# A depthwise convolution on TensorE: two output positions per product, and input copies made of one run per partition

## The chip, the cores and the metric

The kernel runs on one core of one Trainium2 chip. The metric is the device time of one execution in microseconds; before the change three runs gave a median of 1752.48 us (1751.03 to 1752.51). Of one further execution the hardware profiler kept a trace, from which every other time below is taken.

## The reference

One step of a diffusion backbone on 384 tokens (128 of context, 256 of latent) with 1024 channels, in four layers; every layer is a mixer and an MLP. The change touches only the mixer of the second layer, a conformer convolution module:

```python
def _conformer_conv(h, w_pw1, b_pw1, dw_w, dw_b, ln_g, ln_b, w_pw2, b_pw2):
    val, gate = jnp.split(h @ w_pw1 + b_pw1, 2, axis=-1)
    z = val * jax.nn.sigmoid(gate)
    z = _dwconv_centred(z, dw_w, dw_b)          # 31 taps along the tokens, per channel
    z = jax.nn.silu(_layernorm(z, ln_g, ln_b))
    return z @ w_pw2 + b_pw2
```

The two segments of tokens are convolved apart, each padded with zeros. All arithmetic is in float32.

## The kernel before

Channels lie on the 128 partitions in eight tiles (0 to 7), tokens along the free axis; between the two segments is a gap of zeros, so that a tile is 399 columns wide for the convolution. `conformer` goes through the tiles so:

- `pwin(m)` is the product pw1 of tile m, 48 matmuls of 128x128 by 384 columns (value and gate, each with split weights), and `glu(m)` after it: two activations on ScalarE (L834, L835) and a product on VectorE into the padded tile `zp` (L847). Products 0 and 1 come out of the normalisation's own stage, 2 to 7 follow; the text calls them pw2 to pw7.
- Tiles 0 and 1 are convolved on VectorE (`conv_dve`, one instruction of 399 columns per tap, L903), tile 1 in two pieces: 20 taps between pw6 and pw7, the rest after pw7.
- Tiles 2 to 7 are convolved on TensorE (`conv_mm`). A matmul contracts over 128 rows that are 4 shifts of 32 channels; its weights are 32 columns of diagonals from `diag`. Eight steps of four taps, for four groups of 32 channels, make 32 matmuls of 399 columns for a tile. The shifted rows, `z4`, come through DRAM: `zp` is stored to `zd` (L854), and four copies (L857) each fill 32 partitions of `z4` with four runs of 1.7 KB per partition, shifted by one column each. `dg` (L861) brings the tile's 512 KB of diagonals. Stores and copies of tiles 2 to 5 are issued by GpSimd, those of tiles 6 and 7 by SP (`SYNCZ`), which also issues all weight loads, in the order of the program. `z4` has three buffers; `dg` shares three with the modulation weights `dmw`.
- A convolved tile goes from PSUM straight to `zc` with its bias: on ScalarE (L885) for the four tiles in `FIRST`, whose mean over channels `mu` (`shift`) is taken away afterwards, on VectorE (L887) for the others, which subtract `mu` at once. `moments` adds each tile to the running sums for the layer norm.
- Tile 7 is convolved inside `stats`, in 256 and 128 columns; each part is followed by the products `lnm` and `lnv` with ones, which end the sums over channels. Then `normed` normalises all tiles, and the projection pw2 of the module (`out_proj`, product `p`) begins.

An engine takes its instructions in the order of the program, and waits at each until its semaphores are there; that holds for the queues that issue transfers too. A transfer issued by SP or ScalarE signals its landing on one of eight counters (DMAHW0 to DMAHW7 in the orders below), one issued by GpSimd on one of eight others (DMASW0 to 7).

## Time and profile before

| | |
|---|---|
| median of three runs | 1752.48 us |
| the profiled execution | 1750.85 us, with a span of 1748.7 us from the first instruction to the last |
| mean granted clock of TensorE | 0.997 |
| busy, share of the span | TensorE 99%, VectorE 80%, ScalarE 54%, GpSimd 1% |
| moved | 316.69 MB read from HBM, 3.96 MB written, 183 GB/s over the span |
| the convolution on TensorE | group of 448 matmuls, 32.8 us |
| the conformer's stretch from pw2 to the projection | 473.7 to 568.8 us |

Busy time is the time in which an engine had an instruction under way. A row of a timeline gives start, duration, engine, line, operation and tiles (equal neighbours as one row with their count), and in brackets how long the engine was idle ahead of it and what ended that. A row on transfers gives the KB of each and the median time from its issue to its landing. In the windows' table each engine has its busy microseconds and, in brackets, its instructions; then come the clock granted to TensorE (1.00 is full), the busy share of the DMA engines, and what they moved.

### The profile page before, as it was taken

The page shows a single profiled execution, that of the slowest core. Times are in us where ns is not written, and L with a number is a line of the kernel's source. Part 1 is how long each engine was busy: PE and PEld are TensorE (multiplying, and loading weights), DVE is VectorE, ACT ScalarE, POOL GpSimd, SP SyncE. Part 2 cuts the span into 40 slices and gives each one's busy share as a digit, 9 for nine tenths or more (in the row PEclk, how much of TensorE's full clock was granted, in tenths as well). Part 3 has the DMA queues.
Part 4 walks back from the last instruction along what each step waited for, and adds up shares of the span by engine and source line. Part 5 has one row for each costly group of instructions (what it writes and reads, how often), then busy time and mean ns, then how long its engine had stood idle before and what let it go on. Part 6 is the DMA issues. An engine that isn't in the chain of part 4 may idle for free.

```text
span 1748.7 us, 27296 instructions
## 1 busy us (share of the span) xinstructions
PE 1723.2 (99%) x10442; PEld 1625.2 (93%) x10442; DVE 1404.8 (80%) x2791; ACT 945.0 (54%) x1697; POOL 16.1 (1%) x36
## 2 busy tenths in 40 slices
PE   8999999999999999999999999999999999999997
PEld 7779999999986999999987889999999789999997
DVE  5998999899897898889875668889999978843443
ACT  4876672454633774254465657524546976733531
POOL 0000000000020000000000000000000000000000
PEclk9999999999999999999999999999999999999999
DMA  9665367766486247767554433676774413533331
GB/s 389 236 219 177 128 225 254 239 246 236 159 237 180 97 139 259 240 219 241 195 182 140 133 99 130 205 240 235 242 241 162 155 49 121 174 128 121 124 135 43
DMA packets 67795, 322.42 MB, mean 184 GB/s; under 512 B 7952, under 2 KB 13456, under 8 KB 44496
## 3 DMA queue, kind: packets, MB, share of 16 engines
q1 hardware_dynamic: 66384, 316.30, 52.8%
q0 software_dynamic: 1280, 4.38, 1.0%
q8 instruction: 82, 1.34, 0.3%
q14 instruction: 49, 0.40, 0.1%
HBM read 316.69 MB, written 3.96 MB: 183 GB/s over the span
## 4 chain that ended last, share of the span: by engine, by line
PE 77%; DVE 15%; ACT 3%; issue 2%; DMA 2%; SPq 0%; DVEq 0%; ACTq 0%
PE f L131 29%; PE o L131 27%; PE pw L131 4%; PE lo L131 3%; DVE mjunk L331 3%; PE qk L131 3%; DVE wlo L219 2%; PE p L131 2%; PE wo L131 2%; PE cps L131 2%; PE v L131 2%; DVE xf L608 1%; DMA pmw<-wmod 1%; PE s L131 1%; PE po L131 1%
## 5 line engine op out<-in xcount | busy, mean ns | idle before, releaser
L218 ACT ACTIVATE whi<-raw 128x1024 fp32r<-128x1024 f32 x360 | 378.5, 1059 | 545.3 <-PE o L131 327.2
L219 DVE TENSOR_TENSOR wlo<-raw,whi 128x1024 fp32r<-128x1024 f32 x360 | 437.7, 1221 | 165.6 <-ACT whi L218 165.3
L331 DVE SCALAR_TENSOR_TENSOR mjunk<-dmw,condb 128x1024 bf16<-128x1024 f32 x308 | 375.3, 1219 | 1.5
L131 PE MATMUL o<-hl,whi 128*128 128x384 f32 x1024 | 343.0, 335 | 0.0
L131 PE MATMUL o<-hh,wlo 128*128 128x384 f32 x1024 | 343.0, 335 | 0.0
L131 PE MATMUL o<-hh,whi 128*128 128x384 f32 x1024 | 343.0, 335 | 0.0
L131 PEld LDWEIGHTS o<-hh,wlo 128*128 128x128 f32 x1024 | 192.2, 188 | 0.0
L131 PEld LDWEIGHTS o<-hh,whi 128*128 128x128 f32 x1024 | 192.2, 188 | 0.0
L131 PEld LDWEIGHTS o<-hl,whi 128*128 128x128 f32 x1024 | 192.2, 188 | 0.0
L501 DVE SCALAR_TENSOR_TENSOR x<-o,modv,x 128x128 f32<-128x128 f32 (+1 forms) x128 | 47.4, 412 | 69.0 <-PE o L131 69.0
L131 PE MATMUL g<-xf,graw 128*128 128x386 f32 x256 | 85.7, 490 | 1.7 <-DVE gl L666 1.7
L131 PEld LDWEIGHTS g<-xf,graw 128*128 128x128 f32 x256 | 47.9, 190 | 34.3 <-DVE gl L666 2.3
L785 DVE TENSOR_TENSOR hl<-s,hh 128x384 fp32r<-128x384 f32 x128 | 71.1, 555 | 6.6 <-ACT s L784 2.4
L783 ACT ACTIVATE hh<-r 128x384 fp32r<-128x384 f32 x128 | 67.1, 524 | 3.3
L784 ACT ACTIVATE s<-r 128x384 f32<-128x384 f32 x128 | 65.2, 509 | 0.0
L779 ACT ACTIVATE r<-f 128x384 f32<-128x384 f32 x112 | 53.0, 473 | 13.4 <-PE f L131 13.4
L131 PE MATMUL lo<-yh,wlo 128*128 128x384 f32 x128 | 43.5, 340 | 1.6 <-DVE wlo L219 1.6
L131 PE MATMUL lo<-yl,whi 128*128 128x384 f32 x128 | 43.0, 336 | 0.0
L131 PE MATMUL lo<-yh,whi 128*128 128x384 f32 x128 | 42.6, 336 | 0.0
L903 DVE SCALAR_TENSOR_TENSOR zt<-zp,vec,zt 128x399 f32<-128x399 f32 x58 | 36.7, 633 | 1.4
L131 PE MATMUL wo<-oT,whi 128*128 128x384 f32 x128 | 33.7, 343 | 0.0
L131 PE MATMUL cps<-z,dg 128*32 128x399 f32 (+2 forms) x448 | 32.8, 449 | 0.0
(1515 smaller groups left out, 4002.2 us busy)
## 6 DMA issues: line engine op xcount, KB each, us to landing
raw<-wst SPq DMA_DIRECT2D x180, 1024.0 KB, 5.0
dmw<-wmod SPq DMA_DIRECT2D x154, 512.0 KB, 4.1
pmw<-wmod SPq DMA_DIRECT2D x34, 512.0 KB, 6.8
graw<-wst SPq DMA_DIRECT2D x16, 512.0 KB, 4.8
bt<-rpbt SPq DMA_DIRECT2D x16, 384.0 KB, 3.5
z<-zd POOLq DMA_DIRECT2D x16, 213.5 KB, 6.7
dg<-diag SPq DMA_DIRECT2D x6, 512.0 KB, 4.1
pmwl<-wmod SPq DMA_DIRECT2D x4, 512.0 KB, 5.0
```

The costliest lines, as they stand in the source:

```text
L131: i = nc.tensor.matmul(*a, **kw)
L218: nc.scalar.activation(hi, raw[:, s], AF.Copy)
L219: nc.vector.tensor_tensor(lo, raw[:, s], hi.bitcast(F32), op=ALU.subtract)
L331: nc.vector.scalar_tensor_tensor(mjunk, w, 0.5, condb[:, s], op0=ALU.mult, op1=ALU.mult, accum_out=mod_tile(l)[:, c, m, s:s + 1]))
L501: nc.vector.scalar_tensor_tensor(x[m][:, xa:xb], ps[:, a:b], mv[:, g, m, s:s + 1], x[m][:, xa:xb], op0=ALU.mult, op1=ALU.add)
L608: nc.vector.scalar_tensor_tensor(xf, r[:, k:k + LG], lcw[:, j, t, k:k + 1], xf, op0=ALU.mult, op1=ALU.add)
L779: nc.scalar.activation(r, ps[:, :N], AF.Relu)
L783: nc.scalar.activation(hh, r, AF.Square)
L784: nc.scalar.activation(s, r, AF.Square)
L785: nc.vector.tensor_tensor(hl, s, hh.bitcast(F32), op=ALU.subtract)
L903: nc.vector.scalar_tensor_tensor(t, z[:, k:k + CG], dww[:, m, k:k + 1], t, op0=ALU.mult, op1=ALU.add)
```

## The change

Tile 0 stays on VectorE. Tile 1 moves to TensorE, and tiles 1 to 6 (`PAIR_CONV`) get a new form, `conv_pair`: a matmul contracts over 8 shifts of 16 channels, and its 32 output rows are those 16 channels at two neighbouring positions. It has 200 columns (one for each pair of positions), and four steps for eight groups of 16 channels make 32 matmuls for a tile. The weights come from a new input `pairw`. `glu` writes even and odd positions apart; the store to `zd` takes both halves. Channel c*8+g of a tile now sits in row c of group g, so that what a partition of `z4` needs, eight groups one behind the other, is one run of 6.9 KB in DRAM. Eight copies of 16 partitions, one for each shift, fill `z4`. Tile 7 (`LAST`) keeps the old matmuls, but its channels are dealt likewise, and its four copies are of 32 partitions with one run of 6.9 KB each. The rows of the weights, biases and gains that follow are put in the same order ahead of the launch.

The result of a pair product has two positions of a channel on two partitions. ScalarE copies it from PSUM to `co` (L917), four transfers issued by ScalarE (L920, 51 KB each) bring both positions onto one partition in `zq`, and `conv_in` moves it to `zc` (ScalarE for tiles 0 to 3, now in `FIRST`, VectorE for the others). The mean is taken ahead of the end of pw7, three pair products stand ahead of pw6, and three behind pw7. SP issues the copies of tile 5 too.

```diff
-CG = SEQ + 15 + LAT
-CSEG = ((0, 0, SEQ), (1, SEQ + 15, CG))
-CP = CG + CW
-PE_CONV = (2, 3, 4, 5, 6, 7)
+CGAP = 16
+CG = SEQ + CGAP + LAT
+CSEG = ((0, 0, SEQ), (1, SEQ + CGAP, CG))
+CP = CG + CW + 1
+PAIR_CONV = (1, 2, 3, 4, 5, 6)
+LAST = 7
 TAP = CW // 4 + 1
-SYNCZ = (6, 7)
-CONVCUT = 20
+SYNCZ = (5, 6, 7)
 ZW = CG + 4 * (TAP - 1)
+CU = CG // 2
+PV = CU + 15
+PZ = CU + 12
+ZB = 2 * (PV + 1) + 8
+ZT = 3 * CP + ZW
+PT = 7 * PV + PZ
...
-FIRST = (2, 3, 0, 4)
+FIRST = (0, 1, 2, 3)
...
                 for s, a, b in SEG:
-                    o = 15 + 15 * s
-                    i = nc.vector.scalar_tensor_tensor(z[:, a + o:b + o], th[:, a:b], 1.0, v[:, a:b],
-                                                       op0=ALU.add, op1=ALU.mult)
+                    o = 15 + CGAP * s
+                    dst, p, q = z[:, a + o:b + o], th[:, a:b], v[:, a:b]
+                    if m in PAIR_CONV:
+                        o = a // 2 + 8 * s
+                        dst = z[:, 7:7 + 2 * PV + 2].rearrange("p (f v) -> p f v", f=2)[:, :, o:o + (b - a) // 2]
+                        p, q = (t.rearrange("p (v f) -> p f v", f=2) for t in (p, q))
+                    i = nc.vector.scalar_tensor_tensor(dst, p, 1.0, q, op0=ALU.add, op1=ALU.mult)
                 glus.append(i.ins)
-                if m in PE_CONV:
-                    z4 = cp.tile([P, 4, ZW], F32, tag="z4", name=f"z4{l}{m}", bufs=3)
-                    zd = dp.tile([P, CP], F32, tag="zd", name=f"zd{l}{m}", bufs=3)
-                    dma = (nc.sync if m in SYNCZ else nc.gpsimd).dma_start
-                    dma(zd, z)
-                    zg = zd.rearrange("(g c) n -> c g n", g=4)
-                    for s in range(4):
-                        i = dma(z4[32 * s:32 * s + 32], zg[:, :, s:s + ZW])
+                dma = (nc.sync if m in SYNCZ else nc.gpsimd).dma_start
+                if m == LAST or m in PAIR_CONV:
+                    z4 = cp.tile([P, ZT], F32, tag="z4", name=f"z4{l}{m}", bufs=3)
+                    dg = wp.tile([P, D], F32, tag="dmw", name=f"dg{l}{m}", bufs=3)
+                    if m == LAST:
+                        zd = dp.tile([P, CP], F32, name=f"zd{l}{m}")
+                        dma(zd, z[:, :CP])
+                        zr = zd.rearrange("(c g) n -> c (g n)", g=4)
+                        for t in range(4):
+                            i = dma(z4[32 * t:32 * t + 32], zr[:, t:t + ZT])
+                        z4 = [z4[:, g * CP:g * CP + ZW] for g in range(4)]
+                        dg = dg.rearrange("p (t n) -> p t n", t=TAP)
+                        nc.sync.dma_start(dg, diag)
+                    else:
+                        zd = dp.tile([2, P, PV], F32, tag="zd", name=f"zd{l}{m}", bufs=3)
+                        dma(zd.rearrange("f p v -> p f v"), z[:, :2 * PV].rearrange("p (f v) -> p f v", f=2))
+                        for t in range(8):
+                            zr = zd[1 - t % 2].rearrange("(c g) v -> c (g v)", g=8)
+                            i = dma(z4[16 * t:16 * t + 16, :PT], zr[:, t // 2:t // 2 + PT])
+                        z4 = [z4[:, g * PV:g * PV + PZ] for g in range(8)]
+                        dg = dg.rearrange("p (k g n) -> p k g n", k=4, g=8)
+                        nc.sync.dma_start(dg, pairw[PAIR_CONV.index(m)])
                     zds.append(i.ins)
-                    z4s[m] = z4
-                    dgs[m] = wp.tile([P, D], F32, tag="dmw", name=f"dg{l}{m}", bufs=3).rearrange("p (t n) -> p t n", t=TAP)
-                    nc.sync.dma_start(dgs[m], diag[PE_CONV.index(m)])
-
-            z4s, dgs, convs = {}, {}, []
+                    z4s[m], dgs[m] = z4, dg
+
+            z4s, dgs, zqs, evs, convs = {}, {}, {}, {}, []
 
             def pwin(m):
                 keep = {}
@@ -872,19 +897,38 @@
                 for t in range(TAP):
                     for g in range(4):
                         i = matmul(ps[32 * g:32 * g + 32, :], dgs[m][:, t, 32 * g:32 * g + 32],
-                                             z4s[m][:, g, 4 * t + a:4 * t + b], start=t == 0, stop=t == TAP - 1)
+                                             z4s[m][g][:, 4 * t + a:4 * t + b], start=t == 0, stop=t == TAP - 1)
                 convs.append(i.ins)
                 return ps
 
-            def conv_pe(m):
+            def pairs(t, xa, xb):
+                return t[:, xa:xb].rearrange("p (v f) -> p f v", f=2)
+
+            def conv_pair(m):
+                ps = mm_tile(f"cps{l}{m}")[:, :CG].rearrange("p (r u) -> p r u", r=2)
+                for r in range(2):
+                    for k in range(4):
+                        for g in range(4):
+                            i = matmul(ps[32 * g:32 * g + 32, r], dgs[m][:, k, 2 * g + r],
+                                       z4s[m][2 * g + r][:, 4 * k:4 * k + CU], start=k == 0, stop=k == 3)
+                convs.append(i.ins)
+                o = cp.tile([P, 2, CU], F32, tag="co", name=f"co{l}{m}", bufs=2)
+                zq = cp.tile([P, 2, CU], F32, tag="zq", name=f"zq{l}{m}", bufs=2)
+                nc.scalar.activation(o, ps, AF.Copy)
+                for r in range(2):
+                    for f in range(2):
+                        evs[m] = nc.scalar.dma_start(zq[r:P:2, f], o[f:P:2, r]).ins
+                zqs[m] = zq
+
+            def conv_in(m):
                 zcs[m] = zc = cp.tile([P, N], F32, name=f"zc{l}{m}")
-                ps = conv_mm(m, f"cps{l}{m}", 0, CG)
                 for s, a, e in CSEG:
                     _, xa, xb = SEG[s]
+                    src = zqs[m][:, :, a // 2:e // 2]
                     if m in first:
-                        nc.scalar.activation(zc[:, xa:xb], ps[:, a:e], AF.Identity, bias=dwb[:, m:m + 1])
+                        nc.scalar.activation(pairs(zc, xa, xb), src, AF.Identity, bias=dwb[:, m:m + 1])
                     else:
-                        nc.vector.scalar_tensor_tensor(zc[:, xa:xb], ps[:, a:e], dwb[:, m:m + 1], mu[:, xa:xb],
+                        nc.vector.scalar_tensor_tensor(pairs(zc, xa, xb), src, dwb[:, m:m + 1], pairs(mu, xa, xb),
                                                        op0=ALU.add, op1=ALU.subtract)
                 if m not in first:
...
-                    if i > 3:
-                        t = cp.tile([P, 4, ZW], F32, tag="z4", name=f"pmwl{i}", bufs=3)
-                        t = t.rearrange("p a b -> p (a b)")[:, :D]
+                    if i > 2:
+                        t = cp.tile([P, ZT], F32, tag="z4", name=f"pmwl{i}", bufs=3)[:, :D]
                     elif i > 1:
-                        t = cp.tile([P, D], F32, tag="pm", name=f"pmwl{i}", bufs=2)
+                        t = cp.tile([P, D], F32, name=f"pmwl{i}")
                     ready[len(MODS) + i] = mod_load(len(MODS) + i, into=t)
...
             conv_dve(0)
             pwin(3)
             pwin(4)
+            conv_pair(1)
+            conv_pair(2)
+            with tc.issue_after(evs[2]):
+                conv_in(1)
             pwin(5)
-            conv_pe(2)
-            conv_pe(3)
-            lnload(0, 4)
+            conv_pair(3)
+            with tc.issue_after(gvs[-1]):
+                conv_in(2)
+            lnload(0, 3)
             ensure(state["w"] + 3)
             pwin(6)
-            conv_dve(1, 0, CONVCUT)
+            with tc.issue_after(gvs[-1]):
+                conv_in(3)
             ensure(state["w"] + 3)
+            last, (hi, lo) = state["pe"], copied[state["w"]]
+            with tc.issue_after(last), tc.issue_after(hi), tc.issue_after(lo):
+                shift()
             pwin(7)
-            with tc.issue_after(glus[-1]), tc.issue_after(gvs[-1]), tc.issue_after(zds[-1]):
-                conv_dve(1, CONVCUT, CW)
-            conv_pe(4)
-            shift()
-            conv_pe(5)
-            center(1)
-            conv_pe(6)
+            conv_pair(4)
+            conv_pair(5)
+            with tc.issue_after(evs[5]):
+                conv_in(4)
+            preload(AF.Abs_reciprocal_sqrt, zcs[4][:, 0:1])
+            conv_pair(6)
+            with tc.issue_after(evs[6]):
+                conv_in(5)
+                conv_in(6)
             for m in range(KT):
                 for s, a, b in SEG:
                     nc.scalar.activation(x[m][:, a:b], x[m][:, a:b], AF.Identity, bias=gb[:, m, s:s + 1])
-            preload(AF.Abs_reciprocal_sqrt, zcs[6][:, 0:1])
-            lnload(4, LNPRE)
+            lnload(3, LNPRE)
...
-            return out_proj(l, "pw2", j, y, f"p2{l}")
+            with tc.issue_after(zds[-1]), tc.issue_after(ths[5]), tc.issue_after(tvs[5]):
+                return out_proj(l, "pw2", j, y, f"p2{l}")
...
+    turn = np.arange(D).reshape(KT, P)
+    for m in PAIR_CONV:
+        turn[m] = turn[m].reshape(16, 4, 2).transpose(1, 0, 2).reshape(P)
+    turn[LAST] = turn[LAST].reshape(32, 4).T.reshape(P)
+    turn = turn.reshape(D)
...
-    diag = np.zeros((len(PE_CONV), P, TAP, P), f4)
     w = i["conf_dw_w"][0]
+    diag = np.zeros((P, TAP, P), f4)
     ch = np.arange(32)
-    for n, m in enumerate(PE_CONV):
-        for t in range(TAP):
-            for s in range(4):
-                if 4 * t + s < CW:
-                    for g in range(4):
-                        diag[n, 32 * s + ch, t, 32 * g + ch] = w[4 * t + s, m * P + 32 * g + ch]
+    for t in range(TAP):
+        for s in range(4):
+            if 4 * t + s < CW:
+                for g in range(4):
+                    diag[32 * s + ch, t, 32 * g + ch] = w[4 * t + s, LAST * P + 4 * ch + g]
+    pairw = np.zeros((len(PAIR_CONV), P, 4, 8, 32), f4)
+    ch = np.arange(16)
+    for n, m in enumerate(PAIR_CONV):
+        for k in range(4):
+            for t in range(8):
+                for f in range(2):
+                    if 0 <= 8 * k + t - f < CW:
+                        for g in range(8):
+                            pairw[n, 16 * t + ch, k, g, 2 * ch + f] = w[8 * k + t - f, m * P + 8 * ch + g]
```

SP, around tiles 6 and 7 (the two digits ahead of a name's underscore are layer and tile: `zd16` is tile 6's store in layer 1). Before:

```order
L854 DMA zd16_5395<-zp16_4651 128x430 [waits DVE_49,Pool_49]
L857 DMA z416_5394<-zd16_5395 32x4x427 x2
L857 DMA z416_5394<-zd16_5395 32x4x427 [waits DMAHW1_49]
L854 DMA zd17_5492<-zp17_4652 128x430 [waits DMAHW2_49,DVE_49,Pool_49]
L861 DMA dg17_5498<-diag 128x1024 [waits DMAHW3_49,PE_49]
L212 DMA raw59_6094<-wst 128x2048 [waits DMAHW4_49,Activation_49]
L857 DMA z417_5491<-zd17_5492 32x4x427 [waits DMAHW6_49]
L857 DMA z417_5491<-zd17_5492 32x4x427 [waits DMAHW7_49]
L857 DMA z417_5491<-zd17_5492 32x4x427 [waits DMAHW0_49]
```

Neither tile's copies wait here for a transfer of ScalarE. After:

```order
L881 DMA z416_5475<-zd16_5477 16x1717 [waits DMAHW5_49]
L881 DMA z416_5475<-zd16_5477 16x1717 [waits DMAHW7_49]
L881 DMA z416_5475<-zd16_5477 16x1717 [waits DMAHW0_49]
L881 DMA z416_5475<-zd16_5477 16x1717 [waits DMAHW1_49]
L869 DMA zd17_5584<-zp17_4652 128x432 [waits DMAHW2_49,DVE_49,Pool_49]
L875 DMA dg17_5583<-diag 128x1024 [waits DMAHW3_49,PE_49]
L337 DMA dmw95_6605<-wmod 128x1024 [waits DMAHW4_49,PE_49]
L872 DMA z417_5582<-zd17_5584 32x1724 [waits DMAHW6_49]
L872 DMA z417_5582<-zd17_5584 32x1724 [waits DMAHW3_49]
L872 DMA z417_5582<-zd17_5584 32x1724 [waits DMAHW4_49]
```

The copies of tile 6 are eight instead of four (the last four are shown), and tile 7's store stands behind them; a load `dmw95` stands where the weight chunk `raw59` stood.

ScalarE, from the gate of tile 7 on, after the change:

```order
L843 ACTIVATE gth17_5576<-pw17_1_5551,hb1_219 128x384 [waits PE_49]
L844 ACTIVATE gv17_5577<-pw17_0_5526,hb1_219 128x384
L917 ACTIVATE co14_5624<-cps14_5591 128x400 [waits PE_49]
L920 DMA zq14_5625<-co14_5624 64x200 [waits DMAHW5_49,Activation_49]
L920 DMA zq14_5625<-co14_5624 64x200 [waits DMAHW6_49]
L920 DMA zq14_5625<-co14_5624 64x200 [waits DMAHW7_49]
L920 DMA zq14_5625<-co14_5624 64x200 [waits DMAHW0_49]
L917 ACTIVATE co15_5664<-cps15_5631 128x400 [waits PE_49]
L920 DMA zq15_5665<-co15_5664 64x200 [waits DMAHW2_49,Activation_49]
L920 DMA zq15_5665<-co15_5664 64x200 [waits DMAHW3_49]
L920 DMA zq15_5665<-co15_5664 64x200 [waits DMAHW4_49]
L920 DMA zq15_5665<-co15_5664 64x200 [waits DMAHW6_49]
```

Before, no transfer stood here; `zc14` followed `gv17` straight from PSUM. Each transfer takes the counter that it waits for, so the fifth to seventh copies of `z416` follow `zq14`'s first, third and fourth on theirs (5, 7, 0), `zd17` follows `zq15`'s first (2), and the last two copies of `z417` follow `dg17` (3) and `dmw95` (4).

GpSimd's transfers for tiles 1 to 4, after the change:

```order
L878 DMA zd11_4902<-zp11_4646 128x2x215 [waits DVE_49,Pool_49]
L878 DMA zd12_4985<-zp12_4647 128x2x215 [waits DVE_49,Pool_49]
L881 DMA z411_4900<-zd11_4902 16x1717 [waits DMASW0_49]
L881 DMA z411_4900<-zd11_4902 16x1717 x6
L881 DMA z411_4900<-zd11_4902 16x1717 [waits DMASW1_49]
L881 DMA z412_4983<-zd12_4985 16x1717 [waits DMASW2_49]
```

Tile 2's store stands ahead of tile 1's copies, and in the same way tile 4's ahead of tile 3's. Before, tiles 2 and 3 had their four copies right behind their own stores, and tile 5's store stood ahead of tile 4's copies.

30 lines of the change are left out of this document (16 added, 14 removed).

## The prediction

> **What bounds the kernel now.** I began with the page: its first line and the busy times of part 1.
>
> ```profile
> span 1748.7 us, 27296 instructions
> PE 1723.2 (99%) x10442; PEld 1625.2 (93%) x10442; DVE 1404.8 (80%) x2791; ACT 945.0 (54%) x1697; POOL 16.1 (1%) x36
> ```
>
> TensorE is busy for 99% of the span, so work taken from it is time won, if nothing else ends later. But 99% is a mean, so next I cut the conformer's stretch into stages: the products pw2 to pw5, the first two convolved tiles, pw6 and pw7, the other convolutions up to the first layer-norm product (`lnm`), and the normalisation.
>
> ```profile
> core 0: us, PE busy (x) PEld busy (x) DVE busy (x) ACT busy (x) POOL busy (x), PEclk, DMA share, GB/s
> 473.70:506.80 33.10, 33.10 (x193) 33.10 (x192) 30.96 (x59) 19.70 (x34) 6.19 (x11) 1.00 0.76 227
> 506.80:518.00 11.20, 11.20 (x132) 4.18 (x130) 10.80 (x20) 2.73 (x5) 2.75 (x5) 1.00 0.70 211
> 518.00:534.80 16.80, 16.80 (x100) 16.59 (x96) 13.22 (x21) 4.97 (x9) 2.18 (x4) 1.00 0.73 190
> 534.80:557.40 22.60, 22.60 (x265) 9.62 (x264) 18.48 (x36) 8.13 (x15) 0.00 (x0) 1.00 0.75 210
> 557.40:568.80 11.40, 8.54 (x180) 6.93 (x176) 8.34 (x25) 6.48 (x16) 0.00 (x0) 0.99 0.35 130
> ```
>
> Up to 557.4 TensorE never idles: it bounds every stage that the change touches. The copies are always there in time. The timeline of TensorE from the end of pw7 on shows what fills the fourth stage.
>
> ```profile
> 507.11 10.94 PE L131 MATMUL cps<-z,dg 128*32 128x399 f32 x128
> ...
> 534.58 0.34 PE L131 MATMUL pw<-h117h,wlo 128*128 128x384 f32 x1
> 534.85 5.57 PE L131 MATMUL cps<-z,dg 128*32 128x399 f32 x64
> 540.34 2.85 PE L131 MATMUL mu1p<-zc,ones 128*128 128x384 f32 x8
> 543.12 14.39 PE L131 MATMUL cps<-z,dg 128*32 128x399 f32 x192
> 557.44 0.70 PE L131 MATMUL lnm<-me1a,ones 128*128 128x256 f32 x2
> ...
> 559.36 1.96 PE L131 MATMUL cps<-z,dg 128*32 128x128 f32 x64
> ```
>
> I call T the moment at which pw7 ends and the next convolution may start: 534.85 here. From T to `lnm` are 22.6 us of uninterrupted work: tile 4 (5.5), the mean (2.8), tiles 5 and 6 (10.9), 256 columns of tile 7 (14.3 - 10.9, so 3.5).
>
> **The products.** A matmul of 399 columns appears as two records, so a tile is 64 records, 16 rounds of four row groups. The weight loads give the time of a round, and the part of tile 7 with 128 columns gives it for a narrow one.
>
> ```profile
> 507.47 0.13 PEld L131 LDWEIGHTS cps<-z,dg 128*32 128x32 f32 x4 [0.20 <-issue]
> 507.81 0.13 PEld L131 LDWEIGHTS cps<-z,dg 128*32 128x32 f32 x4 [0.20 <-issue]
> ```
>
> A round of 399 columns takes 507.81 - 507.47 = 0.34 us; one of 128 takes 1.96 / 16 = 0.12 (the row at 559.36). On the line between them 200 columns cost 0.12 + 72 x 0.0008 = 0.178, and the 16 rounds of a pair tile 2.9 us, against 5.45. Bounds: 2.0 (as 128 columns) and 5.45. Five full tiles (27.2) become six pair tiles (17.4): TensorE is relieved of 9.8 us. That is the most the change can bring. VectorE loses the 31 taps of tile 1:
>
> ```profile
> L903 DVE SCALAR_TENSOR_TENSOR zt<-zp,vec,zt 128x399 f32<-128x399 f32 x58 | 36.7, 633 | 1.4
> ```
>
> 31 x 0.633 = 19.6 us, worth nothing, since TensorE ran beside it without a gap.
>
> **How T moves.** Ahead of T stood two full tiles (10.9); now stand three pair tiles (8.7) and the mean (2.85). T itself comes 0.7 us later. All gain has to show behind T.
>
> **Waits ahead of T.** Three pair products are wanted early. The first stage gives 33.1 / 4 = 8.28 us for a product, so pw4 ends at 498.5, where conv1 is to start; conv2 follows at 501.4. GpSimd's queue of before shows when copies can go:
>
> ```profile
> 484.79 0.69 POOL L854 DMA_DIRECT2D zd<-zp  x1 [24.87 <-DVE zt L903]
> 487.53 2.19 POOL L857 DMA_DIRECT2D z<-zd  x4 [2.05 <-DMA zd<-zp]
> ...
> 501.44 2.18 POOL L857 DMA_DIRECT2D z<-zd  x4 [7.14 <-DMA zd<-zp]
> 505.32 0.56 POOL L854 DMA_DIRECT2D zd<-zp  x1 [1.70 <-DVE zt L903]
> ```
>
> An issue costs 0.55 us there, and eight copies now cost 4.4 instead of 2.2. In the new order tile 2's store stands ahead of tile 1's copies, so those start where tile 2's started before, at about 487.6, although tile 1 is ready long before. From then on 1.76 MB (two tiles, 128 x 6.9 KB each) have to come in by 501.4, beside two weight chunks. The rates, from the queues and issues of transfers in three windows (516 to 521.5, 486 to 498, 484 to 487) and the page's part 3:
>
> ```profile
> q0 software_dynamic: 287, 0.95, 77.3%
> ...
> raw<-wst SPq DMA_DIRECT2D x2, 1024.0 KB, 8.0
> z<-zd POOLq DMA_DIRECT2D x4, 213.5 KB, 7.0
> ...
> zd<-zp POOLq DMA_DIRECT2D x1, 215.0 KB, 2.4
> ...
> q1 hardware_dynamic: 66384, 316.30, 52.8%
> ```
>
> Copies into 32 partitions moved 0.95 MB in 77.3% of 5.5 us: 223 GB/s. The weights, 128 partitions at a time, moved 316.3 MB in 52.8% of 1748.7 us: 343 GB/s. Copies into 16 partitions are nowhere in this trace. Their runs are four times longer, which may bring them to 343; with half as many partitions they may make only half of 223, about 112. Weights take 2.1 MB / 343 = 6.1 us. conv2's input is then in (with 1.3 us for the last landing) at 487.6 + 6.1 + 1.3 + 5.1 = 500.1 at 343, 502.9 at 223, 510.7 at 112: a wait of 0, 1.5 or 9.3 us. I take 223, the nearest row. conv3: tile 4's store stands ahead of tile 3's copies in the queue; at 505.3 it goes, the eight issues end at 510.3, and the landing takes what this line of the copies' view gives, least, median and longest:
>
> ```profile
> DMA to landing us min/median/max: 3.2/6.6/8.5
> ```
>
> So 513.5 to 517; it is wanted at 501.4 + 1.5 + 2.9 + 8.3 = 514.1. I take 1.0 of 0 to 3. Together 2.5 us (0 to 12).
>
> **Behind T: the queue of SP.** Nothing of this was a wait before: tile 7's store and copies ran in the shadow of 14 us of convolutions.
>
> ```profile
> 533.88 2.11 SPq L857 DMA_DIRECT2D z<-zd  x4
> 537.69 0.34 SPq L854 DMA_DIRECT2D zd<-zp  x1
> 540.47 0.35 SPq L861 DMA_DIRECT2D dg<-diag  x1
> 541.48 1.92 SPq L857 DMA_DIRECT2D z<-zd  x4
> ```
>
> Now that cover is shorter, and the orders shown above add a coupling. Transfers of SP and ScalarE take eight landing counters (DMAHW0 to 7) in turn, and one that reuses a counter waits until the transfer before it on that counter has landed. Tile 6's fifth to seventh input copies take the counters of result copies 1, 3 and 4 of tile 4; tile 7's store takes that of tile 5's first result copy; the third and fourth copies of tile 7 take those of `dg` and `dmw`. All this stands in SP's one queue. The prices:
>
> ```profile
> 535.74 0.56 ACT L834 ACTIVATE gth<-pw,hb 128x384 f32<-128x384 f32 x1
> z<-zd SPq DMA_DIRECT2D x4, 213.5 KB, 4.4
> zd<-zp SPq DMA_DIRECT2D x1, 215.0 KB, 3.3
> dg<-diag SPq DMA_DIRECT2D x1, 512.0 KB, 3.5
> dmw<-wmod SPq DMA_DIRECT2D x154, 512.0 KB, 4.1
> ```
>
> The result copies (51 KB) have no row. The nearest is the 215 KB store's 2.4; half a move less could make it 1.9; from below I allow 1.0, from above 3.3. Taking 2.4:
> conv4 ends at T+2.9, ScalarE's copy at T+3.5, its four issues at 0.33 each run to T+4.9, landed T+6.2 to T+7.3. SP then issues tile 6's last copies to T+7.6; with 3.2 to 4.4 conv6 starts at about T+11, where TensorE has idled since T+5.8. It would end at T+14, or T+15.6 at the low clock that such an idle brings (below).
> conv5 ends at T+5.8, copy T+6.4, first result landed T+9.1: tile 7's store goes at T+9.2 and lands at T+12; `dg` is in at T+13; `dmw`, issued at T+9.9, at T+14. The fourth copy of tile 7 goes at T+14 and lands 4.4 later: T+18.4 (T+17.2 with 3.2, T+20.6 with 6.6). Tile 7 adds 3.5. After such idles the clock is low; the trace has one, ahead of the next projection:
>
> ```profile
> PE p L131 <- ACT yh L407: 2.7, 1, 2.7
> ...
> 568.00:570.00 2.00, 1.20 (x4) 0.66 0.00 0
> 570.00:572.00 2.00, 2.00 (x9) 0.50 0.00 0
> ```
>
> Half clock (third number behind the busy time) for some 3.4 us: 1.7 lost. So `lnm` starts at T+18.4 + 3.5 + 1.7 = T+23.6, against T+22.6: +1.0 (low: 17.2 + 3.5, -1.9; high: +3.2). Tile 6's own results land by T+20 and are summed by T+22, hidden. The normalisation behind `lnm` has the same instructions; a weight conversion that moved into it finds ScalarE idle for 5 of 11.4 us: 0, at most +1.
>
> **Sum.** 0.7 + 2.5 + 1.0 = +4.2 us on the profiled execution's 1750.85, 1755.0; the median of the runs lies 1.6 higher, so **1756.6**. The gain of 9.8 us is thus spent on waits of TensorE for copies, at three places (conv2 and conv3, conv6, tile 7).
>
> **Rival 1: narrow copies run at half rate.** For it: the rows above rank the rates by the partitions written, 343 for 128 and 223 for 32. Against: runs of 1.7 KB may be what slows the latter. Then conv2 waits 9.3, with 1.7 of low clock behind it; conv3's input is in when wanted; tile 6's last 0.44 MB need 2 us more, which SP's queue hands on to tile 7. 0.7 + 9.3 + 1.7 + 1.0 + 2 = +14.7: **1767**, up to 1772 with long landings. The Trainium skill ("SBUF — State Buffer", section "Door 1: The DMA port swizzle") has this as a rule: bandwidth follows how many of 16 ports the partitions reach, 32 neighbouring ones reach 8 and 16 reach only 4. By its table that is about 218 and 109 GB/s; the trace's 223 agrees with the former, no run here shows the latter.
>
> **Rival 2, the other side: the landings are short.** Copies move at 343 (a long run each), so the early waits are 0. Result copies land in 1.0: conv6 starts at T+9.5, tile 7's store goes at T+7.8, `dmw` is in at T+12, the last copy at T+15.2. The idle is then under 3 us; with 0.8 of low clock `lnm` stands at T+19.5: 0.7 - 3.1 = -2.4, **1750**; without any, and with the third and fourth copy not the last to land, -4.5, **1748**. It decides once result copies land in under about 1.5 us. For it: 51 KB is a quarter of the least transfer seen. Against: 215 KB at the 400 GB/s of that store (0.22 MB in 18.3% of 3 us) explains only 0.5 of its 2.4 us.
>
> **Rival 3: a wash.** Copies at 343 and result landings near 2: no early wait, end at -0.5: +0.2, **1752.5**.
>
> **Chances.** Forecast 0.38, rival 1 0.27, rival 2 0.17, rival 3 0.18. About 0.2%, 3.5 us, can be told from no change. The forecast's own range is 1753 to 1762; two thirds of it is beyond 1756. Slower 0.26 + 0.27 = 0.53; faster most of rival 2, 0.15; within 0.2% 0.32. The range reaches from rival 2's better end to beyond rival 1: 1748.3 to 1769.
>
> **What would show it.** Right: TensorE idles ahead of conv6 and tile 7 by 4 to 6 us each, ended by copies `z4`; SP's input copies of tile 6 split in two batches, the second right behind ScalarE's result copies; about 1.5 us idle ahead of conv2; a pair tile takes 2.9 us. Wrong: no idle ahead of conv6; result copies landed in 1 us; an idle of 9 us ahead of conv2 (rival 1); a pair tile over 3.5 us. If `lnm` starts under T+19, I have mispriced the queue.

## The result, and the profile after

The change makes the kernel slower: 1766.26 us median (1764.47 to 1768.87) beside 1752.49 us (1751.03 to 1753.01) for the kernel before, a ratio of 1.0081 with an interval of 1.0064 to 1.0099. The profiled execution took 1764.47 us. I cut both traces at the same four places (S is the start of pw2's products, `p` the first product of the module's projection):

| us | before | after | difference |
|---|---|---|---|
| S to T (end of pw7) | 61.13 | 70.74 | +9.6 |
| T to `lnm` | 22.59 | 26.06 | +3.5 |
| `lnm` to `p` | 11.36 | 11.31 | -0.1 |
| `p` to the end | 1179.90 | 1180.83 | +0.9 |

The last row is a part of the program that the change doesn't touch; in the experiments below it lies between 1178.5 and 1182.2, so 0.9 is scatter. The loss lies in the first two. The page's busy times (the span is 1762.7 us), and the row of TensorE's waits that answers to nothing in the kernel before:

```profile
PE 1720.9 (98%) x10506; PEld 1631.9 (93%) x10506; DVE 1386.5 (79%) x2760; ACT 947.7 (54%) x1703; POOL 23.7 (1%) x52
```

```profile
PE cps L138 <- DMA z<-zd: 16.1, 4, 6.0
```

TensorE's busy time fell by only 2.3 us, and it now waits 16.1 us in four places for the copies that fill `z4`. Its timeline shows the four, and what they do to the work behind them (in order: conv1, conv2, conv3, conv4 with conv5, conv6, the first part of tile 7, `lnm`):

```profile
498.83 2.91 PE L138 MATMUL cps<-z,dg 128*32 128x200 f32 x64
506.12 5.16 PE L138 MATMUL cps<-z,dg 128*32 128x200 f32 x64 [4.38 <-DMA z<-zd]
...
521.95 2.91 PE L138 MATMUL cps<-z,dg 128*32 128x200 f32 x64 [2.14 <-DMA z<-zd]
...
544.50 5.62 PE L138 MATMUL cps<-z,dg 128*32 128x200 f32 x128
556.16 5.56 PE L138 MATMUL cps<-z,dg 128*32 128x200 f32 x64 [6.04 <-DMA z<-zd]
565.28 5.35 PE L138 MATMUL cps<-z,dg 128*32 128x256 f32 x64 [3.55 <-DMA z<-zd]
570.56 0.70 PE L138 MATMUL lnm<-me1a,ones 128*128 128x256 f32 x2
```

A pair tile takes 2.91 us where nothing stood still ahead of it. Behind the idle of 4.38 us the same 64 matmuls take 5.16, and behind 6.04 they take 5.56. The clock explains it, in the table of windows of the same kernel (the first number behind the busy times is the granted clock, then DMA share and GB/s):

```profile
506.20:511.30 5.10, 5.10 (x65) 3.28 (x65) 4.88 (x9) 0.00 (x0) 2.11 (x4) 0.55 0.89 329
```

So T comes later by 4.38 (idle ahead of conv2), 2.25 (conv2 at a clock of 0.55: 5.16 - 2.91), 2.14 (conv3) and 0.65 of work (three pair tiles and the mean against two full tiles), 9.4 of the 9.6 us. The low clock also says why TensorE's busy time fell by only 2.3 us: behind the idles it gives back 2.25 us at conv2, 2.65 at conv6 (5.56 - 2.91) and some 1.8 at tile 7 (5.35 against 3.5).

The other thing to see is the DMA share. Here are the same two windows, the first two rows from the kernel before, the others from the kernel after:

```profile
487.00:507.00 20.00, 20.00 (x117) 19.86 (x115) 18.36 (x28) 6.43 (x9) 5.50 (x10) 1.00 0.92 262
507.00:525.00 18.00, 18.00 (x170) 11.12 (x169) 17.25 (x30) 4.53 (x8) 4.93 (x9) 1.00 0.83 219
```

```profile
487.00:507.00 20.00, 15.62 (x145) 14.22 (x147) 16.29 (x26) 5.81 (x9) 8.49 (x17) 0.92 0.96 238
507.00:525.00 18.00, 15.86 (x172) 13.48 (x162) 9.94 (x16) 5.36 (x10) 8.49 (x17) 0.90 1.00 247
```

Both kernels move 9.2 MB in these 38 us. The engines were already busy for 0.92 and 0.83 of them, and now they are busy for 0.96 and 1.00. So this stretch had little room before the change, which the prediction's longer windows (0.70 to 0.76) did not show.

GpSimd's queue shows how conv3's copies came late:

```profile
494.62 1.71 POOL L881 DMA_DIRECT2D z<-zd  x3 [3.19 <-DMA z<-zd]
...
500.39 0.77 POOL L878 DMA_DIRECT2D zd<-zp  x1 [1.60 <-DVE zt L947]
507.50 0.74 POOL L878 DMA_DIRECT2D zd<-zp  x1 [6.34 <-DVE zt L947]
```

The first row is three of tile 2's copies; ahead of it GpSimd stood still until an earlier copy had landed. The 16 copies of tiles 1 and 2 share GpSimd's eight counters, and from 480 to 530 us its copies waited six times, 7.9 us in all, for earlier copies; in the kernel before they never did. Then come tile 3's store and, 7 us later, tile 4's, which waits for VectorE; only behind that are tile 3's copies issued, at 509.94. The chain of work that ended last, from there on (start, duration, what):

```profile
500.39 9.26 DMA zd<-zp
...
514.90 7.00 DMA z<-zd
...
552.19 3.46 DMA zq<-co
...
555.71 5.43 DMA dmw<-wmod
561.16 4.03 DMA z<-zd
```

Tile 3's store of 215 KB took 9.26 us to land. Behind T the chain runs through conv5, ScalarE's copy to `co`, a result copy, the load `dmw`, the last input copy of tile 7, and tile 7. SP's queue shows the same from its side, and the row of its waits from 538 to 554 us (in all, times, longest) names the cause:

```profile
539.84 13.49 SPq L881 DMA_DIRECT2D z<-zd  x8
553.94 0.34 SPq L869 DMA_DIRECT2D zd<-zp  x1
```

```profile
SPq L881 <- DMA zq<-co: 10.1, 3, 8.0
```

Tile 6's eight input copies stretch over 13.49 us, because the later ones wait on landing counters for ScalarE's result copies; tile 7's store stands behind them. The copies themselves were quick here: they landed in 2.6 to 3.4 us, 16 partitions wide as they are.

### The profile page after: what moved, and what is told of

Read it like the earlier page. It is cut to its first block, busy times and chain, and to the rows that moved or that the text cites. A ratio compares the mean times of both kernels' runs of the same rounds, so it can differ in the third digit from the quotient of the medians.

```text
span 1762.7 us, 27496 instructions
## 1 busy us (share of the span) xinstructions
PE 1720.9 (98%) x10506; PEld 1631.9 (93%) x10506; DVE 1386.5 (79%) x2760; ACT 947.7 (54%) x1703; POOL 23.7 (1%) x52
## 4 chain that ended last, share of the span: by engine, by line
PE 74%; DVE 16%; ACT 4%; DMA 3%; issue 2%; SPq 0%; POOL 0%; ACTq 0%; DVEq 0%
PE f L138 29%; PE o L138 26%; PE lo L138 3%; DVE mjunk L340 3%; PE qk L138 3%; DVE wlo L227 3%; PE p L138 2%; PE wo L138 2%; PE pw L138 2%; PE v L138 2%; DVE xf L617 1%; PE s L138 1%; PE po L138 1%; DVE tr L659 1%; DVE tr L657 1%
## 5 line engine op out<-in xcount | busy, mean ns | idle before, releaser
L510 DVE SCALAR_TENSOR_TENSOR x<-o,modv,x 128x128 f32<-128x128 f32 (+1 forms) x128 | 47.5, 414 | 67.9 <-PE o L138 67.9
L138 PE MATMUL cps<-z,dg 128*32 128x200 f32 (+2 forms) x512 | 29.5, 395 | 16.1 <-DMA z<-zd 16.1
L138 PEld LDWEIGHTS cps<-z,dg 128*32 128x32 f32 x512 | 20.0, 128 | 25.3 <-DMA z<-zd 15.4
```

Of the source, the lines that this page charges most:

```text
L138: i = nc.tensor.matmul(*a, **kw)
L510: nc.vector.scalar_tensor_tensor(x[m][:, xa:xb], ps[:, a:b], mv[:, g, m, s:s + 1], x[m][:, xa:xb], op0=ALU.mult, op1=ALU.add)
```

## The experiments

Three things could make the copies late. (a) They go into 16 partitions, and such copies are slow or fill the DMA engines. (b) It is the bytes: one tile of copies and weights more, and the result copies, beside the same weight chunks. (c) It is order: landing counters shared by SP and ScalarE, stores held in a queue, products placed too early. All runs below carry a ratio to the kernel before, run beside them on the same chip (medians 1750.7 to 1751.2).

**The copies alone.**

> The changed kernel, with the eight copies of 16 partitions of each pair tile merged by twos: four copies of 32 partitions, the same runs of 6.9 KB, the same bytes (the rows of the weights in pairw are swapped by pairs to fit). Narrow-copy theory: with twice the partitions the copies move up to twice as fast, the queue of GpSimd shows over 350 GB/s while busy, or the early idles (4.4 and 2.1 us) vanish; time 1756 or less. Queue and traffic theory: the rate of the copies stays at 190 to 235 GB/s, conv2 still waits 2 to 4 us; half as many transfers loosen the coupling behind T, so that the idle ahead of conv6 falls to under 3 us, while tile 7 still waits for the counter of dmw. Time 1758 to 1763.

```diff
-                        for t in range(8):
-                            zr = zd[1 - t % 2].rearrange("(c g) v -> c (g v)", g=8)
-                            i = dma(z4[16 * t:16 * t + 16, :PT], zr[:, t // 2:t // 2 + PT])
+                        zr = zd.rearrange("f (c g) v -> (f c) (g v)", g=8)
+                        for t in range(4):
+                            i = dma(z4[32 * t:32 * t + 32, :PT], zr[:, t:t + PT])
...
-                            pairw[n, 16 * t + ch, k, g, 2 * ch + f] = ...
+                            pairw[n, 16 * (t ^ 1) + ch, k, g, 2 * ch + f] = ...
```

Each pair of copies becomes one of 32 partitions, so the edit halves their number as well as doubling their width: 1761.59 us, ratio 1.0062 (1.0047 to 1.0077). That is 3.1 us better against its own neighbour (+10.7, not +13.8) and 4.7 by the medians; the two intervals overlap a little. In the trace the stretch from conv1 to `lnm` went from 71.7 to 67.6 us: the idle ahead of conv3 and conv6 is gone, GpSimd's copies no longer wait for one another, and conv2's idle is 3.31. Tile 7's wait grew in their place, as TensorE's timeline shows (conv2 and tile 7):

```profile
507.26 5.56 PE L138 MATMUL cps<-z,dg 128*32 128x200 f32 x64 [3.31 <-DMA z<-zd]
...
562.45 6.23 PE L138 MATMUL cps<-z,dg 128*32 128x256 f32 x64 [10.10 <-DMA z<-zd]
```

Its windows stand beside those of the next run.

**The bytes.**

> The changed kernel, with only half of each weight chunk of the products pw2 to pw7 loaded and used twice: 0.5 MB instead of 1 MB for each of six chunks, every instruction of the engines as it was (this part of the products is left out). It takes traffic away and nothing else. Traffic theory (from 487 to 525 us the DMA engines are full, 92 to 100% busy, so that any copy lands late there): the idle ahead of conv2 falls from 4.4 us to under 1, its low clock with it, that ahead of conv3 from 2.1 to 0, T comes about 8 us earlier, time about 1758; the waits behind T stay. Queue theory (the early copies are late because of the order of GpSimd's queue and its counters): conv2 still waits 3 us or more, time 1764 to 1769.

```diff
-        nc.sync.dma_start(raw, wst[i])
+        few = plan[i][0] == "pw1" and plan[i][-1] > 1
+        nc.sync.dma_start(raw[:, :1024] if few else raw, wst[i, :, :1024] if few else wst[i])
...
-            s = slice(h * 1024, h * 1024 + 1024)
+            s = slice(0, 1024) if few else slice(h * 1024, h * 1024 + 1024)
```

1765.09 us, ratio 1.0085 (1.007 to 1.01): no better than the change, so (b) falls as far as it is about the bytes of the weights. In the trace (of the slowest of four executions, 1769.37 us) conv2 waits 5.44 us, conv1 1.59. The windows of this kernel, 20 and 18 us long, and behind them those of the run with wide copies:

```profile
487.00:507.00 20.00, 16.63 (x144) 15.76 (x142) 17.41 (x27) 7.72 (x12) 9.25 (x18) 1.00 0.95 201
507.00:525.00 18.00, 14.35 (x120) 11.95 (x124) 8.83 (x15) 2.79 (x5) 8.52 (x17) 0.81 0.99 202
```

```profile
487.00:507.00 20.00, 16.95 (x146) 15.74 (x144) 15.58 (x22) 6.18 (x8) 5.38 (x10) 0.98 0.89 241
507.00:525.00 18.00, 17.74 (x180) 14.56 (x181) 12.86 (x21) 6.20 (x11) 4.66 (x9) 0.83 0.92 254
```

With fewer bytes the engines are about as busy as in the change (0.95 and 0.99 against 0.96 and 1.00) and move only some 201 GB/s. In the first window the queue of the weights moved 2.04 MB instead of 2.92, yet took 47.5% of the engines' time instead of 50.2%: the edit took away bytes, but ahead of conv2 hardly any engine time. With wide copies and all the weights they move 241 and 254 at a lower share (0.89, 0.92). So it is the engines' time that is scarce, more than the bytes. What a copy does by itself stands in the queue's row (packets, MB, share of 16 engines) of windows in which little else ran. Here, in the run with half the weights, 514.5 to 519.5, copies into 16 partitions:

```profile
q0 software_dynamic: 205, 0.69, 101.5%
```

0.69 MB in 101.5% of 5 us is 136 GB/s. In the change itself, 517 to 521, beside result copies and weights:

```profile
q0 software_dynamic: 151, 0.52, 79.6%
```

That is 0.52 MB in 79.6% of 4 us, 163 GB/s. And in the run with tile 1 on VectorE (below), 491.5 to 493.5, copies into 32 partitions with the same long runs:

```profile
q0 software_dynamic: 95, 0.49, 107.0%
```

0.49 MB in 107% of 2 us is 229 GB/s, 1.7 times as much. The prediction's 223 was for runs of 1.7 KB, so into 32 partitions a run of 6.9 KB gains next to nothing. These are single short windows. Over the whole of 487 to 507, stores included, the same queue shows a smaller gap, first in the change, then with wide copies:

```profile
q0 software_dynamic: 527, 1.82, 45.5%
```

```profile
q0 software_dynamic: 621, 2.41, 47.6%
```

That is 200 GB/s against 253.

**The counters: no result copies.**

> The changed kernel without the result copies: conv_in reads the products in PSUM as if positions and channels were in place, so co, the 24 transfers of 51 KB (1.2 MB) and ScalarE's issues are left out. Traffic theory: conv2's wait, which comes ahead of any result copy, stays at 3 to 5 us; conv3's goes. Counter theory for what is behind T: SP's queue has no transfers of ScalarE to wait for, conv6 follows conv5 without idle (6.0 us now), tile 7 still waits for the counter of dmw and for the late landing of its own copies, lnm stands at about T+20 instead of T+26. Time about 1758. If conv6 still idles 4 us or more, the counters were not its cause.

```diff
-                o = cp.tile([P, 2, CU], F32, tag="co", name=f"co{l}{m}", bufs=2)
-                zq = cp.tile([P, 2, CU], F32, tag="zq", name=f"zq{l}{m}", bufs=2)
-                nc.scalar.activation(o, ps, AF.Copy)
-                for r in range(2):
-                    for f in range(2):
-                        evs[m] = nc.scalar.dma_start(zq[r:P:2, f], o[f:P:2, r]).ins
-                zqs[m] = zq
+                zqs[m], evs[m] = ps, i.ins
```

1761.59 us, ratio 1.006 (1.0045 to 1.0075). SP's queue, and TensorE's timeline from T on (start, duration):

```profile
543.08 3.75 SPq L881 DMA_DIRECT2D z<-zd  x8
```

```profile
547.78 2.41 PE L138 MATMUL cps<-z,dg 128*32 128x200 f32 x52
549.67 6.44 PE L138 MATMUL cps<-z,dg 128*32 128x200 f32 x147
562.56 5.07 PE L138 MATMUL cps<-z,dg 128*32 128x256 f32 x64 [6.45 <-DMA z<-zd]
```

Tile 6's eight copies are issued in 3.75 us instead of 13.49, and conv4 to conv6 run in one piece (the first two rows, one stretch): the waits for ScalarE's transfers made conv6's wait. This kernel also leaves out the 1.2 MB that those transfers move; but in the change tile 6's copies landed in 2.6 to 3.4 us once issued, so behind T it was the counters and not the traffic. `lnm` starts at T+19.8 instead of T+26.1. Ahead of T nothing is won: conv2 waits 5.95 us for the narrow copies, conv3 2.84 for ScalarE. So of the change's tail 6.3 us belong to the result copies, and yet the kernel is still slower than before.

**The order, in three ways.** GpSimd issues the copies of tiles 6 and 7:

> The changed kernel, with the stores and copies of tiles 6 and 7 issued by GpSimd instead of SP; nothing else. GpSimd's transfers have counters of their own, so neither ScalarE's result copies nor the loads dg and dmw stand ahead of these copies any more. Queue theory (the late waits come from SP's queue and its shared counters): the idle ahead of conv6 falls from 6.0 us to under 1, that ahead of tile 7 stays at 3 to 4 us, and lnm starts at about T+17 instead of T+26.1; the early waits stay. Time 1766.3 - 9 = about 1757. Narrow-copy theory (rival 1: copies into 16 partitions are themselves slow): the copies are as slow from another queue, TensorE still idles over 4 us ahead of conv6, time 1764 to 1768.

```diff
-SYNCZ = (5, 6, 7)
+SYNCZ = (5,)
```

1768.85 us, ratio 1.0102 (1.0086 to 1.0119), and not the gain that was expected. The tail is T+25.4; conv6 still waits 4.90, where under 1 was expected. GpSimd sends tile 6's copies only from T-1.8 on, behind tile 6's store, where SP began at T-4.7 in the change. SP, free of the copies, ran ahead with its weight loads, and GpSimd's store and copies of tile 7 landed in 8.07 and 6.35 us. The run also tells about scatter: its order up to conv2 is that of the change, and there conv2 waited 4.38 us.

```profile
509.29 4.17 PE L138 MATMUL cps<-z,dg 128*32 128x200 f32 x64 [7.41 <-DMA z<-zd]
```

conv1 and conv2 behind pw5, conv3 behind pw6:

> The changed kernel, with conv1 and conv2 behind pw5 (8.3 us later on TensorE) and conv3 behind pw6; nothing else. If the early loss (4.4 us ahead of conv2, 2.3 us of low clock in it, 2.1 us ahead of conv3) is a matter of when the copies land, it disappears, since the copies of tile 2 had landed at 506.1 and conv2 would now start at about 510: T comes 8 to 9 us earlier, time about 1758. If instead the wait only moves (tile 4's copies wait for the buffer that conv1 frees, the copies of tile 3 land still later), T gains under 3 us and the time stays above 1763. The late waits should stay as they are in either case.

```diff
-            conv_pair(1)
-            conv_pair(2)
-            with tc.issue_after(evs[2]):
-                conv_in(1)
             pwin(5)
-            conv_pair(3)
+            conv_pair(1)
+            conv_pair(2)
+            with tc.issue_after(evs[2]):
+                conv_in(1)
...
             pwin(6)
+            conv_pair(3)
```

1770.7 us, ratio 1.0113 (1.0096 to 1.0129). conv1 and conv2 no longer wait, but others do:

```profile
534.35 1.01 PE L138 MATMUL mu1p<-zc,ones 128*128 128x384 f32 x1 [4.03 <-ACT zc L929]
...
562.48 5.56 PE L138 MATMUL cps<-z,dg 128*32 128x200 f32 x64 [8.37 <-DMA dg<-pairw]
```

The mean needs tiles 1 to 3, and the result copies of the first two, 51 KB each, now take 7.6 to 10.0 us to land; tile 6's weights come late too. The wait moved, and grew.

All three edits (wide copies, later products, GpSimd for tiles 6 and 7):

> The three edits of the runs before this one together: conv1 and conv2 behind pw5, tiles 6 and 7 issued by GpSimd, four copies of 32 partitions. Queue theory: no early idle, none ahead of conv6, under 4 us ahead of tile 7; then the relief of TensorE shows: 1752.5 + 0.7 - 5 = about 1748, faster than the kernel before. If the 9.8 us taken from TensorE are not real, or if other work becomes the bound, it stays at 1752 or above.

1768.64 us, ratio 1.0103 (1.0088 to 1.0118): worse than the wide copies alone. The mean waits three times (3.81, 1.88, 3.82), tile 7 7.48.

**One link of the tail.** Wide copies, and the load `dmw95` put behind tile 7's copies:

> Four copies of 32 partitions as in e3_copies32, and the loads dmw95 and dmw96 behind tile 7's copies in SP's queue instead of ahead of them. Counter theory: tile 7's idle falls from the 10.1 us of e3_copies32 to 3 to 5 us, since its third copy no longer waits until dmw has landed; lnm about 6 us earlier; time 1755 (1753 to 1757) against 1761.6. Traffic theory, if it holds behind T too: the copies are as late without dmw, the idle stays at 8 us or more, time 1760 to 1762.

```diff
+            state["hold"] = zds[-1]
             stats(1)
...
-            nc.sync.dma_start(w, wmod[i])
+            with tc.issue_after(state["hold"]):
+                nc.sync.dma_start(w, wmod[i])
```

1759.87 us, ratio 1.0049 (1.0033 to 1.0066). Tile 7's wait fell from 10.10 to 8.60 only, not to the 3 to 5 us expected. The chain that ended last:

```profile
551.47 4.42 DMA zq<-co
...
556.25 3.99 DMA z<-zd
```

With `dmw` gone, a result copy of tile 5 holds the counter itself. Taking out one holder hands the wait to the next.

**Tile 1 back on VectorE.** The same, with the old home of tile 1, conv2 and conv3 behind pw5, conv4 behind pw6, conv5 and conv6 behind pw7:

> e7_copies32_dmw_behind with tile 1 back on VectorE in two pieces, as in the kernel before, so five pair tiles: conv2 and conv3 behind pw5, conv4 behind pw6, conv5, conv6 and tile 7 behind pw7. It takes 1.8 MB of copies, weights and results from the full stretch and 2.9 us from TensorE. Traffic theory: no wait ahead of T, T at +0.7 against the kernel before; conv5 and conv6 run to T+5.8, tile 7's copies are in at about T+12, lnm at T+17 against T+22.6: time 1752 - 5 = about 1747 (1744 to 1750), faster than the kernel before. If VectorE, with tile 1's taps back, now ends the sums later than tile 7 (its busy share was 80%), 1751 or more.

```diff
-PAIR_CONV = (1, 2, 3, 4, 5, 6)
+PAIR_CONV = (2, 3, 4, 5, 6)
+CONVCUT = 20
...
-FIRST = (0, 1, 2, 3)
+FIRST = (0, 2, 3, 4)
...
+            pwin(5)
+            conv_pair(2)
             conv_pair(3)
...
             pwin(6)
+            conv_pair(4)
...
+            conv_dve(1, 0, CONVCUT)
...
             pwin(7)
+                conv_dve(1, CONVCUT, CW)
+                center(1)
-            conv_pair(4)
             conv_pair(5)
             conv_pair(6)
```

1750.16 us, ratio 0.9996 (0.9987 to 1.0005): the time of the kernel before, 9.7 us better than the run before this one. No product ahead of T waits for its copies, and T stands at 536.92. This is the best version, and TensorE has 12.7 us less convolution in it than the kernel before (five full tiles of 5.45 are five pair tiles of 2.91), yet nothing is gained. Its timeline and chain say why:

```profile
551.91 5.70 PE L139 MATMUL cps<-z,dg 128*32 128x256 f32 x64 [9.37 <-DMA z<-zd]
```

```profile
539.83 3.51 DMA zd<-zp
...
543.50 3.12 DMA z<-zd
546.64 5.13 DMA z<-zd
```

conv5 and conv6 end at T+5.6. Tile 7 starts at T+15.0: its gate ends 2.9 us behind T, the store takes 3.51, and the last copy goes only when an earlier one has landed after 3.12 us, and itself lands in 5.13. The chain from pw7 to tile 7 through DRAM takes 15 us here, and TensorE has work for 5.6 of them. In the kernel before, tile 7's copies were issued from 541.48 on and landed in 6.3 to 8.4 us, so they were in between T+14 and T+16.5; TensorE had 19.1 us of convolutions and mean to do meanwhile, and never saw the chain.

With narrow copies and `dmw95` in its old place, the rest as in the last run:

> The changed kernel with tile 1 alone put back on VectorE in two pieces (and conv2 and conv3 behind pw5, conv4 behind pw6, the mean from tiles 0, 2, 3 and 4): still eight copies of 16 partitions for a pair tile, still dmw ahead of tile 7's copies. If one tile too many for the transfers of the stretch is most of the loss, the early idles go as in e8_tile1_on_vectore and the time is 1752 or less. If narrow copies (136 GB/s while alone, 229 for 32 partitions) and SP's counters cost by themselves, conv6 and tile 7 still wait and lnm stands at about T+24: time 1755 to 1758.

1772.12 us, ratio 1.0109 (1.0094 to 1.0124), the slowest of all. TensorE's timeline at conv3, and GpSimd's queue:

```profile
522.09 4.81 PE L139 MATMUL cps<-z,dg 128*32 128x200 f32 x64 [11.81 <-DMA zq<-co]
```

```profile
507.06 0.74 POOL L879 DMA_DIRECT2D zd<-zp  x1 [10.92 <-DVE zt L948]
```

The order of GpSimd's queue came out differently: tile 4's store, which waits 10.92 us for VectorE, stands ahead of tile 3's copies; these were issued until 512.2 and took mostly over 10 us to land, and conv3 started at 522.1 (the row names a result copy, which landed at the same time). So moving tile 1 alone doesn't give the last run's gain. The two runs differ in width, in the place of `dmw95` and in this order, and I can't share the 22 us out among them.

**Work to fill the tail.** Three more versions put pair products where tile 7 waits. conv3 to conv6 behind pw7, tile 1 on VectorE, the mean from tiles 0 and 2, wide copies, tile 6 issued by GpSimd:

> A try for a version that beats both: e8_tile1_on_vectore, but only conv2 ahead of pw7 (behind pw5) and conv3 to conv6 behind it, so that TensorE has 11.6 us of work while tile 7's store and copies are under way, which took 15 us from T in e8 (TensorE idled 9.4 us there); the mean comes from tiles 0 and 2 alone, and tile 6's store and copies are issued by GpSimd, so that SP has only tile 7's. T comes 10.9 - 2.9 - 1.4 = 6.6 us earlier than before, lnm at T+20 (15 for the copies, 3.5 for tile 7, up to 1.7 of low clock): 9 us earlier, time about 1742 (1740 to 1747). Against it: VectorE was busy 73 of the 84 us from 473.7 to 557.4 and keeps all of tile 1; if it ends the sums, only 3 to 5 us are won, 1746 to 1748.

1762.32 us, ratio 1.0062 (1.005 to 1.0075). The same with conv3 between pw6 and pw7:

> As e10_filler_behind_pw7, with conv3 behind pw6 instead of behind pw7. T comes 2.9 us later than there, and TensorE has 8.7 us of work behind it for a wait of 15: lnm 2.9 us later than in e10, time about 1745. If VectorE is what ends the sums in e10, no difference to it.

1753.99 us, ratio 1.0015 (1.0007 to 1.0024). From TensorE's timelines and the chains that ended last, first of the former, then of the latter:

```profile
566.76 1.19 PE L139 MATMUL lnm<-me1a,ones 128*128 128x256 f32 x2 [8.04 <-DVE me1a L386]
```

```profile
557.11 8.04 DMA zq<-co
```

```profile
549.47 5.55 PE L139 MATMUL cps<-z,dg 128*32 128x256 f32 x64 [8.64 <-DMA z<-zd]
558.83 0.67 PE L139 MATMUL lnm<-me1a,ones 128*128 128x256 f32 x2 [3.81 <-DVE me1a L386]
```

```profile
549.34 7.98 DMA zq<-co
```

In the former tile 7 is done 8.04 us ahead of `lnm`, which waits for VectorE's sums; in the latter tile 7's copies and the sums share the wait. VectorE was feared as the next bound, but it stands idle itself ahead of its last sum, 5.98 and 5.43 us, for a result copy of tile 6 that lands in 8.04 and 7.98 us. The result copies end last, not VectorE's taps.

Last, without tile 1's taps on VectorE: six pair tiles, wide copies, `dmw95` behind, conv1 behind pw5, conv2 and conv3 behind pw6, conv4 to conv6 behind pw7, the mean from tile 0 alone:

> A last try to beat both with tile 1 on TensorE, so with six pair tiles: copies of 32 partitions, dmw behind tile 7's copies, conv1 behind pw5, conv2 and conv3 behind pw6, conv4 to conv6 behind pw7, the mean from tile 0 alone (which needs no result copy). VectorE is no longer full as in e10 and e11. If the transfers of the stretch keep up (conv2 and conv3 without idle, since their inputs landed by 507 and 521 in e3), T comes at 534, tile 7's copies are in at T+15, lnm at about T+20 = 554 against 557.4: time about 1748 (1745 to 1750). If the transfers bound the stretch, as the earlier runs with six pair tiles suggest (1760 to 1769), TensorE idles ahead of conv1 to conv3 or in pw7 by more than 4 us, or tile 7's copies are later than T+17, and the time is 1754 to 1762.

1756.6 us, ratio 1.0032 (1.0021 to 1.0043). TensorE waits only 0.3 us up to T (534.05), and then three times: 4.55 ahead of conv5, 5.31 ahead of conv6, 2.63 ahead of tile 7. In the chain stands

```profile
513.28 14.94 DMA zq<-co
```

a result copy of 51 KB that landed in 15 us. No version beat the kernel before.

## Why the prediction was right, and where its sizes were wrong

The direction and the mechanism held: the work taken from TensorE came back as waits for copies, at conv2, conv3, conv6 and tile 7, and the chain behind T (conv5, result copy, `dmw`, tile 7's last copy) runs through the transfers that were forecast. The size did not hold: +4.2 us was forecast for the profiled execution, +13.6 came (1764.47 - 1750.85). The measured 1766 lies outside the forecast's own 1753 to 1762, and inside the wider range only because that was drawn to take in rival 1. By its steps:

- *The products.* Right: 2.91 us for a pair tile where 2.9 was worked out. No run shows a gain from VectorE's relief, which was costed at nothing.
- *How T moves.* Right: 0.65 us of work against 0.7.
- *Waits ahead of T* is the step that failed by most: 2.5 us forecast, 8.8 measured (6.5 idle, 2.25 low clock; the bound was 12). Four things were wrong in it. The copies were priced at 223 GB/s, the rate of 32 partitions; 16 partitions alone ran at 136, at 163 beside other transfers, and over 487 to 507 the queue made 200. The 1.3 us for the last landing is shown by no row. The copies' issue was priced without a pause; GpSimd waited 7.9 us for its own counters. Tile 3's store was not priced as a wait: it took 9.26 us to land (stores issued by GpSimd took 2.4 to 7.4 in the kernel before), and tile 4's store, ahead of the copies, went at 507.5 instead of 505.3. And the low clock behind conv2's idle stood in rival 1, but not in the forecast.
- *Behind T* was mis-sized: +1.0 forecast, +3.5 measured. conv6 started at T+11.7 (T+11 forecast), tile 7's store went at T+9.4 (T+9.2). `dmw` went at T+11.2 instead of T+9.9: it waited for tile 5's third result copy on its own counter, which the forecast had only standing ahead of it in the queue. ScalarE's transfers took 0.61 us each to issue, not SP's 0.33, and that result copy landed in 3.46, not 2.4. `dmw` itself took 5.43, not 4.1; the last copy 4.03, not 4.4. That 4.4 came so near is luck: it was the landing of tile 6's copies in the kernel before, where tile 7's own took 6.3 to 8.4. Together 1.3 + 1.3 - 0.4 = 2.2 of the 2.4 us by which tile 7 started later than forecast.
- *Rival 1* (narrow copies at half rate) came closer in time, 1767, with part of its mechanism. The rate is 0.59 of the wide one; its idle of 9.3 us ahead of conv2 was 4.4 here and 7.4 in the run with the same order. Wide copies, with half the number of transfers, take back 3 to 5 us of the 13.8, so width is a part at most, not the whole; behind T the narrow copies landed in 2.6 to 3.4 us. The Trainium skill ("SBUF — State Buffer", section "Door 1: The DMA port swizzle") gave about 218 and 109 GB/s for 32 and 16 neighbouring partitions; 229 agrees with the first, and 136 lies above the second. The measurement decides. That copies to two different groups of partitions were in flight at once may explain it; that is argued, not shown.
- *Rival 2* is out: result copies landed in 3.46 us where it needed 1.5, and conv2 and conv3 waited. With no result copies at all the kernel was still slower than before, so even landing in no time would not have brought its 1748.
- *The signs.* Idles ahead of conv6 and tile 7 (6.0 and 3.6, forecast 4 to 6), tile 6's copies held for ScalarE's result copies, 2.9 us for a pair tile: all there. The idle ahead of conv2 was 4.4 instead of 1.5.

Where the 9.8 us of relief went is answered by the run with tile 1 on VectorE. In the kernel before, 19.1 us of work between T and tile 7 covered a chain of 14 to 16.5 us from the gate of tile 7 through DRAM to its matmuls. With 5.6 us of work and a chain of 15 TensorE stood still for the difference; with the gap filled by other pair tiles, their result copies ended last instead.

Open: why a result copy lands in 1.7 us at one time and in 9 to 15 at another (full engines are the likely reason, but no run changed that alone), and how the 22 us between the best and the worst run divide among width, counters and queue order.

## What to carry to other kernels

Before making an engine's work shorter, measure the longest chain that runs in its shadow, through stores, copies and counters: below that length the saved time turns into idle, and then into low clock. Price a transfer at the rate of its own shape, and where several run at once, by the engine time that they fill and not by their bytes. Transfers of two queues that share landing counters wait for each other in program order, and taking out one holder hands the wait to the next.
